# Sixteen modulation blocks as columns on TensorE: stationary weights and a one-column moving operand in place of a broadcast gate product

## The chip, the cores and the metric

The kernel runs on one NeuronCore of one Trainium2 chip. The metric is the device time in microseconds of one execution; three runs of the kernel before gave a median of 2649.09 us (2648.99 to 2653.47).

## What is computed

Two transformer stacks run one after the other on 256 positions of width 1024, in float32. The first stack has two layers with adaptive modulation; only its first layer matters here:

```python
c_act = silu(c)                                   # (1, 1024)
mod = c_act @ ada_w[i] + ada_b[i]                 # (1, 6144)
sh_m, sc_m, gt_m, sh_f, sc_f, gt_f = split(mod, 6)
h = rmsnorm(x, g0) * (1 + sc_m) + sh_m
y = rglru_mixer(h, ...)                           # layer 0
x = x + gt_m * rmsnorm(y, g1)                     # first gate
h = rmsnorm(x, g2) * (1 + sc_f) + sh_f            # shift and scale of the first conv FFN
y = conv_ffn(h, ...)
x = x + gt_f * rmsnorm(y, g3)
```

The 6144 modulation values of a layer are 48 blocks of 128: blocks 0 to 7 are `sh_m`, 8 to 15 `sc_m`, 16 to 23 `gt_m`, 24 to 31 `sh_f`, 32 to 39 `sc_f`, 40 to 47 `gt_f`. A block is a product of a 1024-vector with a 1024 by 128 piece of `ada_w`, 512 KB in float32.

## The kernel before, in words

**Products of the stacks.** Weights come from one packed array in chunks of 512 KB (`Weights._raw`, L360, tile `raw`, four buffers). Most are split into a high and a low part, `hi` by ScalarE (L372) and `lo` by VectorE (L373), in nine buffers each, and a product is three TensorE passes (L439 to L441 for `mm_b`, 512 moving columns; L446 to L448 for `mm_a`, 256 moving columns). A plain float32 matmul, as in the lines below, shows as two matmul records and two weight loads in the profile.

**Modulation blocks on VectorE.** `ada_step` (L502) loads a transposed 128 by 1024 block (L508, tile `adar`, two buffers, or `adag` where `more` is set) and makes one multiply with accumulation against `silu(c)` broadcast to 128 partitions (`cact`; L510). The result is one column of `dot[i]`. The factor 2 left out of `silu` is put right by 0.5 in `mods` (L521). Blocks 0 to 15 of layer 0 are made in `rg_x`, two per step of a loop over eight 128-row slices of the input, as they are needed. The rest are made in the background: `bg(n)` (L1012) spreads `DUE` blocks over a stage, 16 in the first stage (`rg`), 28 in the first conv FFN.

**The first gate on TensorE.** Blocks 16 to 23 are not made that way. `rg_x` transposes `cact` eight times (L577) and copies the result to `crep` (L578): the vector along the partitions, repeated over 128 columns. `gate0` (L598) then multiplies `crep` (stationary) with eight 128 by 1024 pieces of `ada_w` (tile `adag`, two buffers, L611), 512 moving columns at a time (L613, 16 matmuls, accumulating in two `y` banks), adds the bias with two matmuls of one partition (L616), and VectorE scales both halves with `norm_g` (L617) into `row0`, a row already spread over 128 partitions.

**Other gates** are made by `gate_row` (L619) from columns: eight diagonal tiles `dg` on VectorE (L632, two buffers), eight 128 by 128 float32 matmuls with a tile of ones (L633) and two copies on ScalarE (L634).

**The first stage, `rg` (L802).** In order: `rg_x`; the depthwise convolution of its result (L831, L833); a loop over four groups `g` that takes two steps of `gate0`, then two gate products of 16 matmul records each (L850), their tanh and exp, and background blocks; square roots and scans (L873 to L876); a loop over eight columns blocks `j` of the gate branch (`up`, L446 to L448, 24 records per `j`, GeLU L884, split L451 and L452); the output projection (L439 to L441); then `turn`, which uses the gate row at L654 and the next layer's shift and scale in `pre` (L686, L688).

**Order.** A scheduler orders each engine's queue by readiness in its own model and by program order; calls wrapped in `keep_in_program_order` stay in order among themselves. All loads go through SyncE's one queue. TensorE, VectorE and SyncE execute their queues in order, so what waits at the head holds what stands behind it.

Of the kernel before, what the change touches and what calls it, by code (L numbers as in the profile page):

```python
# [8 lines left out]
F32 = mybir.dt.float32  # L9
F32R = mybir.dt.float32r  # L10
I32 = mybir.dt.int32
AF = mybir.ActivationFunctionType
OP = mybir.AluOpType
# [3 lines left out]
D = 1024  # L17
# [11 lines left out]
OVER = 4  # L29
LEAD, LATE = 4, 7  # L30

DUE = {(0, 0): 16, (0, 1): 28, (1, 0): 18, (1, 1): 10}

# [33 lines left out]
def _rows(w):  # L69

    return np.concatenate([w[k * 128:(k + 1) * 128] for k in range(w.shape[0] // 128)], 1)
# [194 lines left out]
def _host(inputs, stages1, stages2):  # L266
    p = {k: np.asarray(v) for k, v in inputs.items()}
    arr = {}
    pieces = []
    for st in stages1 + stages2:  # L270
        pieces += _pieces_stage(st, p)
    arr["w"] = _pack(pieces)
    plan = [(k, a.shape[1]) for k, a in pieces]
    arr["x"] = np.ascontiguousarray(p["x"][0])
    cols = _Cols()
    if stages1:
        arr["c"] = np.ascontiguousarray(p["c"])
        order = {0: [j for k in range(8) for j in (k, 8 + k)] + list(range(16, 48)), 1: list(range(48))}
        ada = []
        for i in range(2):  # L280
            t = p["ada_w"][i].T.reshape(48, 128, D)
            ada.append(t[order[i]])
        arr["ada"] = np.ascontiguousarray(np.stack(ada))
        arr["adag"] = np.ascontiguousarray(p["ada_w"][0][:, 2 * D:3 * D]).reshape(8, 128, D)
        arr["gateb"] = np.ascontiguousarray(np.stack([p["ada_b"][0][2 * D:3 * D], p["norm_g"][0, 1]]))
        for i in range(2):
            cols.add(f"ada_b{i}", p["ada_b"][i])
            for n in range(4):
                cols.add(f"norm_g{i}{n}", p["norm_g"][i, n])
            for n in range(3):  # L290
                cols.add(f"cf_w{i}{n}", p["ffn_conv_w"][i, n])
            cols.add(f"cf_b{i}", p["ffn_conv_b"][i])
        for n in range(4):
            cols.add(f"rg_w{n}", p["rg_conv_w"][0, n])
        for nm in ("rg_conv_b", "rg_ba", "rg_bx", "rg_lambda", "gla_b_alpha"):
            cols.add(nm, p[nm][0])
        arr["walpha"] = np.ascontiguousarray(p["gla_w_alpha"][0])
        arr["gla_g"] = np.ascontiguousarray(p["gla_norm_g"])
        ii = np.arange(128)
        m = np.zeros((128, 8, 128), np.int32)  # L300
        for l in range(7):
            s = 64 >> l
            m[:, l, :] = ((ii[:, None] // (2 * s) == ii[None, :] // (2 * s))
                          & (ii[:, None] // s % 2 == 0) & (ii[None, :] // s % 2 == 1))
        m[:, 7, :] = np.eye(128, dtype=np.int32)
        arr["glamask"] = m
        arr["cols"] = np.ascontiguousarray(np.concatenate(cols.parts, 1))
    if stages2:
        arr["lngb"] = np.ascontiguousarray(np.stack([p["ln_g_2"], p["ln_b_2"]], 2).reshape(12, 2, D))
        arr["fox_b"] = np.ascontiguousarray(p["fox_b_f_2"])  # L310
        arr["mla_g"] = _colv(np.concatenate([p["mla_q_norm_g_2"][0], p["mla_kv_norm_g_2"][0]]))
        ii = np.arange(128)
        cm = np.zeros((128, 256), np.float32)
        cm[:, 128:] = np.where(ii[:, None] >= ii[None, :], 0.0, NEG)
        arr["cmask"] = cm
        arr["tri"] = (ii[:, None] <= ii[None, :]).astype(np.float32)
        tabs = []
        for dim in (16, 32):
            inv = np.float32(500000.0) ** (-np.arange(0, dim, 2, dtype=np.float32) / np.float32(dim))
            ang = np.arange(S, dtype=np.float32)[:, None] * inv[None, :].astype(np.float32)  # L320
            co, si = np.cos(ang), np.sin(ang)
            tabs.append(np.concatenate([co, co, -si, si], 1))
        arr["rope"] = np.ascontiguousarray(np.concatenate(tabs, 1).astype(np.float32))
    return arr, plan, cols.at
# [150 lines left out]
class Block1:  # L475
# [9 lines left out]
    def ada_init(self):  # L485
        nc, Q = self.nc, self.Q
        c = Q.tile([128, D], F32, name="cact")
        nc.sync.dma_start(out=c, in_=self.a["c"][0].partition_broadcast(128))
        self.cols = Q.tile([128, self.a["cols"].shape[1]], F32, name="cols")
        nc.sync.dma_start(out=self.cols, in_=self.a["cols"])  # L490
        th = Q.tile([128, D], F32, name="adar", tag="adar", bufs=2)
        self.ACT.activation(out=th, in_=c, func=AF.Tanh, scale=0.5)
        self.V.scalar_tensor_tensor(out=c, in0=th, scalar=1.0, in1=c, op0=OP.add, op1=OP.mult)
        self.cact = c
        self.dot = [Q.tile([128, 48], F32, name=f"dot{i}") for i in range(2)]
        self.mod = [Q.tile([128, 48], F32, name=f"mod{i}") for i in range(2)]
        self.order = {0: [j for k in range(8) for j in (k, 8 + k)] + list(range(16, 48)), 1: list(range(48))}

        self.todo = [(i, b) for i in range(2) for b in range(48) if i or not 16 <= b < 24]
        self.done = set()  # L500

    def ada_step(self, pin=False, more=False):  # L502
        if not self.todo:
# [56 lines left out]
    def rg_x(self):  # L560


        k, nc, V = self.k, self.nc, self.V
        xn = self.normed()
        xT = self.R.tile([128, 8, 256], F32, name="xnT", tag="big0", bufs=1)
        for kk in range(0, 8, 2):
# [2 lines left out]
                for t in range(2):  # L569
                    nc.tensor.transpose(p[:, q, t * 128:t * 128 + 128], xn[t][:, (kk + q) * 128:(kk + q + 1) * 128], k.ident)  # L570
            self.ACT.copy(out=xT[:, kk:kk + 2, :], in_=p)

        self.crep = self.R.tile([128, 8, 128], F32, name="crep", tag="crep", bufs=1)
        for q in range(0, 8, 4):
            p = k.bank("u", 4, (128, 4, 128))
            for j in range(4):
                nc.tensor.transpose(p[:, j, :], self.cact[:, (q + j) * 128:(q + j + 1) * 128], k.ident)  # L577
            self.ACT.copy(out=self.crep[:, q:q + 4, :], in_=p)  # L578
        acc = [k.bank("y" if j < 4 else "u", 4) for j in range(8)]
        h = self.h_tiles()  # L580
        mod, dot = self.mod[0], self.dot[0]
# [13 lines left out]
                    nc.tensor.matmul(acc[n * 4 + j][:, :256], w[:, j * 128:j * 128 + 128], f, start=kk == 0, stop=kk == 7)  # L595
        return h, acc

    def gate0(self):  # L598

        k, Q, R, nc = self.k, self.Q, self.R, self.nc  # L600
        two = R.tile([1, 128], F32, name="two", tag="two", bufs=1)
        self.V.memset(two, 2.0)
        b = Q.tile([1, D], F32, name="gb0", tag="xn", bufs=2)
        k.tc.keep_in_program_order(nc.sync.dma_start(out=b, in_=self.a["gateb"][0:1]))
        self.row0 = Q.tile([128, D], F32, name="grow", tag="grow", bufs=1)
        k.tc.keep_in_program_order(nc.sync.dma_start(out=self.row0, in_=self.a["gateb"][1].partition_broadcast(128)))
        p = [k.bank("y", 4) for _ in range(2)]
        half = [slice(n * 512, n * 512 + 512) for n in range(2)]
        for kk in range(8):
            w = R.tile([128, D], F32, name="adag", tag="adag", bufs=2)  # L610
            k.tc.keep_in_program_order(nc.sync.dma_start(out=w, in_=self.a["adag"][kk]))  # L611
            for n in range(2):
                nc.tensor.matmul(p[n], self.crep[:, kk, :], w[:, half[n]], start=kk == 0, stop=False)  # L613
            yield
        for n in range(2):
            nc.tensor.matmul(p[n], two, b[:, half[n]], start=False, stop=True)  # L616
            self.V.scalar_tensor_tensor(out=self.row0[:, half[n]], in0=p[n], scalar=0.5, in1=self.row0[:, half[n]], op0=OP.mult, op1=OP.mult)  # L617

    def gate_row(self, i, w):  # L619

        if (i, w) == (0, 0):
            return self.row0
        k, Q = self.k, self.Q
        m = self.mods(i, 3 * w + 2)
        gc = k.small("gc", 8)
# [176 lines left out]
    def rg(self):  # L802
# [32 lines left out]


        au = []
        gate0 = self.gate0()
        for g in range(4):
            gates = []  # L840
            next(gate0)
            next(gate0)
            for q, nm in enumerate(("wa", "wx")):
                w = k.whole(f"rg.{nm}.{g}")
                u = k.bank("u", 4, (128, 2, 256))
# [20 lines left out]
            V.scalar_tensor_tensor(out=xg, in0=ig, scalar=1.0, in1=xg, op0=OP.add, op1=OP.mult)  # L866
            au.append((d, r, xg))
            self.bg(6)
        for _ in gate0:
            pass  # L870
        for g in range(4):
            d, m, xg = au[g]
            k.tc.keep_in_program_order(ACT.activation(out=m, in_=m, func=AF.Sqrt, scale=-0.25))  # L873
# [4 lines left out]
        xhi = R.tile([128, 8, 256], F32R, name="xchi", tag="big1", bufs=1)  # L878
        xlo = R.tile([128, 8, 256], F32R, name="xclo", tag="big2", bufs=1)
        for j in range(8):  # L880
            u = k.bank("u", 4)
            self.up(u[:, :256], f"rg.g.{j}", x)
            ge = n2("wx")[:, :256]
            k.tc.keep_in_program_order(ACT.activation(out=ge, in_=u[:, :256], func=AF.Gelu_apprx_tanh))  # L884
            V.tensor_tensor(out=xc[:, j, :], in0=ge, in1=xc[:, j, :], op=OP.mult)
            k.split(xhi[:, j, :], xlo[:, j, :], xc[:, j, :])
            self.bg(24)
# [132 lines left out]
    def run(self):  # L1020
# [5 lines left out]
        for st in k.stages1:  # L1026
# [6 lines left out]
                self.pre(0, mods, x)  # L1033
                end = [1, mods, x]
            with k.tc.tile_pool(name=f"st_{st[0]}{i}", bufs=1) as self.R:
                k.pad(self.R, st[0], 40)
                stage = self.rg() if st[0] == "rg" else self.gla(x) if st[0] == "gla" else self.conv_ffn(i, x)
                if st[0] != "rg":

# [540 lines left out]
```

## Time and profile before

| | |
|---|---|
| median of three runs | 2649.09 us |
| the profiled execution | 2656.96 us |
| its span, first to last instruction | 2655.2 us |
| TensorE busy in the span | 98% |
| VectorE busy | 72% |
| ScalarE busy | 53% |
| bytes moved by DMA | 514.39 MB |

The profiled execution took 7.87 us (0.3%) more than the median; 1.8 us of its time lie outside the span. Busy time of TensorE is modelled (a matmul's end overlaps the next one's start), so the pace of matmuls is read from start to start, and idle time from the waits.

### The profile page before, as it was taken

Reading aid. Unit: us, or ns where it says so; the run is one execution under the profiler, and the core shown is the slowest. Engines: PE = TensorE matmul, PEld = TensorE weight load, DVE = VectorE, ACT = ScalarE, POOL = GpSimd, SP = SyncE. Lnnn points to the kernel's source line nnn. Section 1 sums busy time; section 2 is a strip of 40 time slices with the busy share of each in tenths; the row PEclk is TensorE's granted clock in tenths of the full one; section 3 lists DMA queues with packets and bytes.
Section 4 is the critical chain, followed back from the end, with each engine's and each line's share of the span. In section 5 each row is a group of like instructions: output and inputs, shape, how many; then the busy total and the mean of one; then the engine's idle time right before and its main releaser. Section 6 shows DMA issues by size and latency. Waiting matters only on the chain.

```text
span 2655.2 us, 44259 instructions
## 1 busy us (share of the span) xinstructions
PE 2591.1 (98%) x16680; PEld 2289.2 (86%) x16680; DVE 1918.3 (72%) x3876; ACT 1414.8 (53%) x2848; POOL 77.8 (3%) x115
## 2 busy tenths in 40 slices
PE   7899998999999999999999999999999999999998
PEld 5689887899899779989987899899889989977897
DVE  6889888887666886676666855766885676687755
ACT  4665564766554655444555544544754455456542
POOL 0000010000000000000000000000000000000000
PEclk9999999999999999999999999999999999999999
DMA  8878674665765537666654565665455565453652
GB/s 315 301 245 304 220 253 158 226 211 162 223 192 168 166 118 232 195 185 207 192 174 126 186 187 175 215 192 158 153 175 191 177 214 195 154 188 115 222 188 91
DMA packets 141082, 514.39 MB, mean 194 GB/s; under 512 B 16178, under 2 KB 16562, under 8 KB 139331
## 3 DMA queue, kind: packets, MB, share of 16 engines
q1 hardware_dynamic: 140866, 511.56, 59.9%
q8 instruction: 131, 2.15, 0.3%
q14 instruction: 85, 0.69, 0.1%
HBM read 510.44 MB, written 1.05 MB: 193 GB/s over the span
## 4 chain that ended last, share of the span: by engine, by line
PE 78%; DVE 8%; issue 8%; DMA 3%; ACT 2%; POOL 1%; DVEq 0%; POOLq 0%; SPq 0%; ACTq 0%
PE u L446 11%; PE u L448 11%; PE u L447 11%; PE y L441 10%; PE y L440 10%; PE y L439 10%; DVE lo L373 3%; PE u L439 2%; PE u L441 2%; PE u L440 2%; DMA raw<-w 2%; PE u L1232 1%; PE u L470 1%; PE u L1259 1%; PE u L1251 1%
## 5 line engine op out<-in xcount | busy, mean ns | idle before, releaser
L373 DVE TENSOR_TENSOR lo<-raw,hi 128x512 fp32r<-128x512 f32 (+4 forms) x1501 | 1080.8, 746 | 500.1 <-ACT hi L372 488.5
L372 ACT CAST hi<-raw 128x512 fp32r<-128x512 f32 (+4 forms) x1501 | 952.2, 667 | 735.3 <-issue 411.0
L446 PE MATMUL u<-hThi,hi 128*128 128x256 f32 x3016 | 841.1, 279 | 3.2 <-ACT hi L372 1.4
L447 PE MATMUL u<-hTlo,hi 128*128 128x256 f32 x3016 | 838.4, 278 | 0.0
L448 PE MATMUL u<-hThi,lo 128*128 128x256 f32 x3016 | 837.9, 278 | 0.2 <-DVE lo L373 0.2
L446 PEld LDWEIGHTS u<-hThi,hi 128*128 128x128 f32 x3016 | 566.8, 188 | 7.9 <-ACT hi L372 1.6
L447 PEld LDWEIGHTS u<-hTlo,hi 128*128 128x128 f32 x3016 | 567.2, 188 | 4.5 <-issue 1.0
L448 PEld LDWEIGHTS u<-hThi,lo 128*128 128x128 f32 x3016 | 568.9, 189 | 0.5 <-DVE lo L373 0.4
L441 PE MATMUL y<-hi,hT 128*128 128x512 f32 x704 | 276.9, 393 | 0.0
L440 PE MATMUL y<-lo,hT 128*128 128x512 f32 x704 | 276.5, 393 | 0.0
L439 PE MATMUL y<-hi,hT 128*128 128x512 f32 x704 | 274.4, 390 | 0.0
L439 PE MATMUL y<-hi,hThi 128*128 128x512 f32 (+6 forms) x504 | 189.5, 377 | 0.9 <-ACT hThi L451 0.8
L440 PE MATMUL y<-lo,hThi 128*128 128x512 f32 (+6 forms) x504 | 185.8, 370 | 0.0
L441 PE MATMUL y<-hi,hTlo 128*128 128x512 f32 (+6 forms) x504 | 185.0, 371 | 0.2 <-DVE hTlo L452 0.2
L440 PEld LDWEIGHTS y<-lo,hT 128*128 128x128 f32 x704 | 132.2, 188 | 27.4
L439 PEld LDWEIGHTS y<-hi,hT 128*128 128x128 f32 x704 | 132.2, 188 | 27.3
L441 PEld LDWEIGHTS y<-hi,hT 128*128 128x128 f32 x704 | 132.3, 188 | 27.0
L439 PE MATMUL u<-hi,hThi 128*128 128x512 f32 x320 | 127.2, 399 | 1.6 <-ACT hThi L451 1.6
L451 ACT CAST hT<-th 128x256 fp32r<-128x256 f32 x144 | 58.4, 406 | 130.5 <-DVE th L1119 130.5
L440 PE MATMUL u<-lo,hThi 128*128 128x512 f32 x320 | 125.5, 393 | 0.0
L441 PE MATMUL u<-hi,hTlo 128*128 128x512 f32 x320 | 124.5, 394 | 0.0
L439 PEld LDWEIGHTS y<-hi,hThi 128*128 128x128 f32 x504 | 94.9, 188 | 18.7 <-ACT hThi L451 2.3
(301 smaller groups left out, 3122.8 us busy)
## 6 DMA issues: line engine op xcount, KB each, us to landing
raw<-w SPq DMA_DIRECT2D x823, 512.0 KB, 3.8
adar<-ada SPq DMA_DIRECT2D x80, 512.0 KB, 4.8
gb<-lngb SPq DMA_DIRECT2D x12, 1024.0 KB, 4.8
adag<-ada SPq DMA_DIRECT2D x8, 512.0 KB, 5.4
adag<-adag SPq DMA_DIRECT2D x8, 512.0 KB, 6.2
raw<-w SPq DMA_DIRECT2D x8, 384.0 KB, 3.0
raw<-w SPq DMA_DIRECT2D x5, 480.0 KB, 3.7
raw<-w SPq DMA_DIRECT2D x4, 396.0 KB, 3.0
```

What stands on the lines that cost most here:

```text
L372: nc.scalar.copy(out=hi[:, a:b], in_=r[:, a:b])
L373: nc.vector.tensor_tensor(out=lo[:, a:b], in0=r[:, a:b], in1=hi[:, a:b].bitcast(F32), op=OP.subtract)
L439: mm(out, xhi, w[0], start=start, stop=False)
L440: mm(out, xhi, w[1], start=False, stop=False)
L441: mm(out, xlo, w[0], start=False, stop=stop)
L446: mm(out, whi, xhi, start=start, stop=False)
L447: mm(out, whi, xlo, start=False, stop=False)
L448: mm(out, wlo, xhi, start=False, stop=stop)
L451: self.nc.scalar.copy(out=hi, in_=src)
L470: self.nc.tensor.transpose(p[:, k * 128:k * 128 + 128], x[:, (h + k) * 128:(h + k + 1) * 128], self.ident)
L1232: nc.tensor.matmul(scores[e], qh(e), kh(e), start=True, stop=True)
L1251: nc.tensor.transpose(pt[:, e, j, :], probs[e0 + e][:, j * 128:j * 128 + 128], k.ident)
```

## The change

The product with `crep` goes, with its transposes, its copies, the bias matmuls and the bias and norm arrays. Blocks 16 to 31, the first gate and the shift of the first conv FFN, are made by TensorE as columns: `silu(c)` is held as eight columns (`ccol`), a block's 1024 by 128 piece of weights is the stationary operand, eight 128 by 128 tiles of it, and one column of `ccol` is the moving operand. Eight blocks share a PSUM bank and are copied to `dot` together. Eight blocks run in the loop over `g` (two per group), eight in the loop over `j` (one per column block). The first gate's row is made by `gate_row` at `j == 2`. VectorE's background share of the first stage falls from 16 blocks to 8.

```diff
-DUE = {(0, 0): 16, (0, 1): 28, (1, 0): 18, (1, 1): 10}
+PEADA = (16, 32)
+ROWAT = 2
+DUE = {(0, 0): 40 - PEADA[1], (0, 1): 28, (1, 0): 18, (1, 1): 10}
...
-        arr["adag"] = np.ascontiguousarray(p["ada_w"][0][:, 2 * D:3 * D]).reshape(8, 128, D)
-        arr["gateb"] = np.ascontiguousarray(np.stack([p["ada_b"][0][2 * D:3 * D], p["norm_g"][0, 1]]))
+        arr["adag"] = np.ascontiguousarray(np.stack([
+            _rows(p["ada_w"][0][:, j * 128:j * 128 + 128]) for j in range(PEADA[0], PEADA[1])]))
...
+        cols.add("c", p["c"][0])
...
-        self.todo = [(i, b) for i in range(2) for b in range(48) if i or not 16 <= b < 24]
-        self.done = set()
+        self.ccol = Q.tile([128, 8], F32, name="ccol")
+        self.ACT.activation(out=self.ccol, in_=self.col("c", 0, 8), func=AF.Tanh, scale=0.5)
+        self.V.scalar_tensor_tensor(out=self.ccol, in0=self.ccol, scalar=1.0, in1=self.col("c", 0, 8), op0=OP.add, op1=OP.mult)
+        self.todo = [(i, b) for i in range(2) for b in range(48) if i or not PEADA[0] <= b < PEADA[1]]
+        self.done, self.rows = set(), {}
...
-        self.crep = self.R.tile([128, 8, 128], F32, name="crep", tag="crep", bufs=1)
-        for q in range(0, 8, 4):
-            p = k.bank("u", 4, (128, 4, 128))
-            for j in range(4):
-                nc.tensor.transpose(p[:, j, :], self.cact[:, (q + j) * 128:(q + j + 1) * 128], k.ident)
-            self.ACT.copy(out=self.crep[:, q:q + 4, :], in_=p)
...
-    def gate0(self):
...
+    def pe_ada(self):
+
+        k, nc = self.k, self.nc
+        p = None
+        for j in range(*PEADA):
+            w = self.R.tile([128, D], F32, name="adag", tag="adag", bufs=2)
+            k.tc.keep_in_program_order(nc.sync.dma_start(out=w, in_=self.a["adag"][j - PEADA[0]]))
+            if j % 8 == 0:
+                p = k.bank("y", 4, (128, 512))
+            for kk in range(8):
+                nc.tensor.matmul(p[:, j % 8:j % 8 + 1], w[:, kk * 128:kk * 128 + 128], self.ccol[:, kk:kk + 1], start=kk == 0, stop=kk == 7)
+            if j % 8 == 7:
+                self.V.tensor_copy(self.dot[0][:, j - 7:j + 1], p[:, :8])
+                self.done |= {(0, b) for b in range(j - 7, j + 1)}
             yield
...
     def gate_row(self, i, w):
 
-        if (i, w) == (0, 0):
-            return self.row0
+        if (i, w) in self.rows:
+            return self.rows.pop((i, w))
...
-        gate0 = self.gate0()
+        pe = self.pe_ada()
         for g in range(4):
             gates = []
-            next(gate0)
-            next(gate0)
+            next(pe)
+            next(pe)
...
-        for _ in gate0:
-            pass
...
         for j in range(8):
+            next(pe, None)
+            if j == ROWAT:
+                self.rows[0, 0] = self.gate_row(0, 0)
             u = k.bank("u", 4)
             self.up(u[:, :256], f"rg.g.{j}", x)
...
-                k.pad(self.R, st[0], 40)
+                k.pad(self.R, st[0], 24)
```

## Rows read from the trace of the kernel before

**Rows 1.** The page's first part: busy time of each engine in the span.

```profile
PE 2591.1 (98%) x16680; PEld 2289.2 (86%) x16680; DVE 1918.3 (72%) x3876; ACT 1414.8 (53%) x2848; POOL 77.8 (3%) x115
```

**Rows 2.** Stretches: us, busy PE, PEld, DVE, ACT, POOL; granted clock, DMA share, GB/s.

```profile
50.50:84.00 33.50, 27.63 (x91) 17.78 (x89) 25.33 (x47) 22.99 (x47) 0.00 (x0) 0.90 0.83 303
84.00:140.00 56.00, 51.22 (x304) 42.07 (x303) 51.32 (x81) 31.48 (x53) 3.42 (x6) 1.00 0.86 293
340.00:2655.20 2315.20, 2282.66 (x14859) 2025.35 (x14857) 1632.43 (x3355) 1220.44 (x2523) 64.62 (x85) 1.00 0.57 182
```

**Rows 3.** What TensorE waited for, 50 to 84 us, then 84 to 140 us.

```profile
PE y L613 <- DMA adag<-adag: 4.9, 1, 4.9
...
PE u L682 <- DVE xn L677: 1.7, 1, 1.7
PE y L440 <- DVE lo L373: 1.6, 3, 1.0
PE u L446 <- ACT hi L372: 1.4, 1, 1.4
```

**Rows 4.** TensorE's instructions in order of time (start, us, line, count, idle before).

```profile
50.56 3.65 PE L613 MATMUL y<-adag,crep 128*128 128x512 f32 x8
58.74 3.60 PE L613 MATMUL y<-adag,crep 128*128 128x512 f32 x8
62.18 10.52 PE L850 MATMUL u<-xc,raw 128*128 128x256 f32 x48
77.57 6.75 PE L613 MATMUL y<-adag,crep 128*128 128x512 f32 x8 [4.87 <-DMA adag<-adag]
83.76 0.68 PE L446 MATMUL u<-hThi,hi 128*128 128x256 f32 x1
...
95.22 1.98 PE L616 MATMUL y<-gb,two 1*128 1x512 f32 x4
97.13 0.38 PE L447 MATMUL u<-hTlo,hi 128*128 128x256 f32 x1
```

**Rows 5.** SyncE's queue in order of time, then median landing time of those loads.

```profile
64.91 4.70 SPq L360 DMA_DIRECT2D raw<-w  x3
70.53 0.90 SPq L611 DMA_DIRECT2D adag<-adag  x2
...
adag<-adag SPq DMA_DIRECT2D x8, 512.0 KB, 6.2
```

**Rows 6.** Weight loads in order of time, two products of 16 moving columns.

```profile
1380.19 0.42 PEld L1426 LDWEIGHTS u<-lf,ones 128*128 128x128 f32 x2
1380.54 0.30 PEld L1427 LDWEIGHTS u<-lf,tri 128*128 128x128 f32 x2
1380.76 0.19 PEld L439 LDWEIGHTS y<-hi,hThi 128*128 128x128 f32 x1
```

**Rows 7.** Weight loads in order of time: at full clock, then at half clock.

```profile
400.91 1.87 PEld L969 LDWEIGHTS u<-F 128*128 128x128 f32 x16
402.70 0.19 PEld L441 LDWEIGHTS y<-hi,hTlo 128*128 128x128 f32 x1
...
436.11 3.12 PEld L971 LDWEIGHTS u<-qT,kT 128*128 128x128 f32 x16
```

**Rows 8.** VectorE: one block, the gate's last step, and the diagonal tiles.

```profile
96.43 1.22 DVE L510 SCALAR_TENSOR_TENSOR adar<-adar,cact 128x1024 f32<-128x1024 f32 x1
97.58 1.28 DVE L617 SCALAR_TENSOR_TENSOR grow<-y,grow 128x512 f32<-128x512 f32 x2
...
L632 DVE TENSOR_SCALAR dg<-ident,gc x24: 277/286/290, 277.7 to 654.1; 128x128 f32<-128x128 f32 x24
```

**Rows 9.** A stretch behind TensorE's wait (columns as in group 2).

```profile
78.00:80.00 2.00, 2.00 (x3) 0.75 (x3) 2.00 (x4) 0.48 (x1) 0.00 (x0) 0.50 0.75 240
```

**Rows 10.** ScalarE in order of time: copies of the vector, the next step.

```profile
15.45 1.12 ACT L578 COPY crep<-u 128x512 f32<-128x512 f32 x2 [0.27 <-PE u L577]
17.28 0.60 ACT L555 ACTIVATE hf<-xnT,mod,A 128x256 f32<-128x256 f32 x1 [0.71 <-DVE lam L818]
```

More of the change, by code (lines that the diff above doesn't have):

```diff
@@ L596, in rg_x @@
         return h, acc
-    def gate0(self):
[L600 to L613, printed above, removed]
+    def pe_ada(self):
[11 more added lines that the diff above has]
+                self.done |= {(0, b) for b in range(j - 7, j + 1)}
             yield
-        for n in range(2):
-            nc.tensor.matmul(p[n], two, b[:, half[n]], start=False, stop=True)
-            self.V.scalar_tensor_tensor(out=self.row0[:, half[n]], in0=p[n], scalar=0.5, in1=self.row0[:, half[n]], op0=OP.mult, op1=OP.mult)
     def gate_row(self, i, w):
-        if (i, w) == (0, 0):
-            return self.row0
+        if (i, w) in self.rows:
+            return self.rows.pop((i, w))
         k, Q = self.k, self.Q
```

## The prediction, made before the changed kernel was run

> **What bounds the kernel now.** I read the page's busy times first, then the busy times by stretch, then what TensorE waited for, then its instructions in order of time. The reader should see that TensorE is the bound nearly everywhere: 98% busy over the span [rows 1], and after 340 us 2282.7 of 2315.2 us [rows 2]. A delay of TensorE in the first stage has no slack behind it that could take it up, so it arrives at the end nearly whole.
>
> The change touches two stretches. From 50.5 to 84 us (the loop over `g`) TensorE's work and gaps alternate: three pairs of gate steps, the four group products, and one wait of 4.87 us for a load of `adag`, after which the engine ran its eight records from 77.57 to 83.76 us instead of in some 3.4 us [rows 4]; the granted clock in that stretch is 0.50, the 1.2 GHz level [rows 9]. From 84 to 140 us (the loop over `j`, the output projection, the first turn) TensorE waited 1.7 + 1.6 + 1.4 us and some tenths [rows 3]; the rest is back-to-back work. VectorE is 51.3 of 56 us busy there [rows 2], about as full, but TensorE's waits on it are only the 1.7 + 1.6 us. So work put on TensorE here costs its full length, and work taken from VectorE gives back at most the waits.
>
> **What goes from TensorE.** Sixteen gate matmuls of 512 columns show as 32 records. A pair of steps is eight records; from 58.74 to 62.18 us that is 3.44 us, 0.43 us each [rows 4]. At full clock 32 x 0.43 = 13.8 us. The bias matmuls run from 95.22 to 97.13 us, 1.9 us [rows 4]. Together 15.7 us. The eight transposes and, behind them, the two copies of the vector end before 17.28 us, where ScalarE's next step waited 0.71 us for VectorE [rows 10]: they lie beside other work and count nothing either way. In the same place the new tanh and multiply on eight columns are two tiny instructions; I count 0, at most some tenths.
>
> **What comes to TensorE.** Sixteen blocks of eight float32 matmuls are 128 matmuls, 256 records, each with a fresh 128 by 128 weight load. No row has one moving column. The nearest has 16: its four weight loads run from 1380.19, with the third at 1380.54 and the next line's at 1380.76, so 0.11 us from load to load [rows 6]. With 128 columns it is (402.70 - 400.91) / 16 = 0.112 us [rows 7]. The pace does not fall from 128 columns to 16, so the weight load sets it and one column should not help: 256 x 0.112 = 28.7 us. The ends: 0.06 us a record if the load can be had at about half that price (nothing here shows it), 15.4 us; and 0.195 us, the pace of the same shapes at half clock (3.12 / 16) [rows 7], 49.9 us. I take 0.112, which both rows give.
>
> The Trainium skill, page "TensorE: Matmul & The Clock Gate", section "Back-to-back issue gap", puts a matmul of 1 to 64 columns at about 25 ns; by that the blocks would be an estimated 256 x 0.025 = 6.4 us. The loads of [rows 6] speak against it at 0.11 us, and the same page's section on LDWEIGHTS makes the load depend on its columns alone, which the trace agrees with. The sum doesn't use it.
>
> The row at `j == 2` adds eight 128-column float32 matmuls, 16 records, 16 x 0.112 = 1.8 us. Its diagonal tiles come two at a time from VectorE at 0.29 us each [rows 8]; if VectorE is late TensorE waits. I add 0.7 us for that, 0 to 3.
>
> So TensorE's own work grows by 28.7 + 1.8 - 15.7 = **14.8 us**.
>
> **What VectorE and the loads give back.** VectorE loses eight blocks at 1.15 us each (96.43 to 97.58, where the next line starts) and the gate's last step, 1.2 us [rows 8], 10.4 us; it gains eight diagonal tiles at 0.25 to 0.29 us and five tiny steps, about 3 us. The net 7 us matters only through TensorE's waits. The bytes stay: eight loads of 512 KB move from VectorE's blocks to TensorE's, and one broadcast of 512 KB goes. Their place changes: in the loop over `g` SyncE has some five fewer `adar` loads ahead of or among the `adag` loads. In the kernel before the third pair was issued only at 70.53 us, behind three `raw` loads that held the queue 4.70 us, and landed 7 us later [rows 4, 5]. Fewer loads that wait for VectorE should bring it earlier. What can come back: the wait, 4.9 us, the half-clock excess, 6.2 - 3.4 = 2.7 us, and up to 3.2 us of waits on `hi` and `lo` between 84 and 140 us: 10.8 us in all. Half of the first two and a third of the last is my value, 3.8 + 1.0 = 4.8 us, 0 and 10.8 the ends; the `raw` loads still hold the queue.
>
> Then the sum: 14.8 + 0.7 - 4.8 = **+10.7 us**, taken as +10. Against the profiled execution that is 2656.96 + 10 = 2667; that execution is 7.9 us over the median of the runs, so in the metric 2649.1 + 10 = **2659 us**. The ends of this case: 14.8 - 10.8 = +4 and 14.8 + 0.7 = +15.5, 2653 to 2665.
>
> **Queues that are moved past.** SyncE is the one to watch. In the loop over `j` it now has eight `adag` loads between the weight loads. Each waits until TensorE has finished the block two before it, and behind it stand the `raw` loads that feed `hi` and `lo`. Block to block is 24 records at 0.117 us plus 1.8 us, 4.6 us, so a load has 2 x 4.6 - 1.8 = 7.4 us to land; the median landing is 6.2 us [rows 5]. It fits, with little to spare. VectorE's copy of eight columns and the row's tiles stand in its queue among the splits; the row is used only at the turn, after the output projection, and the shift later still, so neither is late. GpSimd's queue is not touched.
>
> **Rivals.**
>
> *One: the clock falls in the blocks.* One moving column for each load leaves the array almost without work, and a pair of blocks in the loop over `g` is 3.6 us long. After the wait of 4.87 us the clock was at 0.50 for the next six microseconds [rows 4, 9]. If a stretch of one-column matmuls is treated like a wait, the blocks go from 0.112 to 0.195 us a record: half of them so is 128 x 0.083 = +11 us on top of the first sum, 2670; all, with the group products behind them slowed, some +25 us, 2684. Against it: the engine is never without an instruction, and single blocks in the loop over `j` stand between dense products. 18%.
>
> *Two: a new wait takes the place of the old.* TensorE meets a block whose load has not landed. The price of one such wait is in the trace: 4.9 us and 2.7 us of half clock. Two more of them than I counted give 2659 + 15 = 2674; eight waits of 1 us give 2667. The 7.4 us against 6.2 us above is what decides. 12%.
>
> *Three, the other side: the record is cheaper than its load looks.* If a record costs c, TensorE's growth is 272c - 15.7 (with the row at the same pace), and with all 10.8 us given back the change breaks even at c = 26.5 / 272 = 0.097 us and is faster by more than 0.2% (5.3 us) below 0.078 us. At 0.06 us it is 16.3 - 15.7 - 10.8 = -10 us, 2639. For it: every load in the trace stands beside at least 16 columns, and VectorE, relieved by 7 us where it is 92% busy, may free more than the waits I can see. Against it: rows 6 and 7 give the same pace at 16 and 128 columns. By the Trainium skill's 25 ns (the same section) it would end at an estimated 2631. 22%: 14 with the time below -0.2%, 8 within.
>
> **How the numbers follow.** First sum 48%, rivals 18, 12 and 22%. About 0.2% of the time, 5.3 us, is what a measurement of this kernel can tell from no change. Of the first sum 8 points lie below +5.3 us. So faster 0.14, same 0.08 + 0.08 = 0.16, slower 0.40 + 0.18 + 0.12 = 0.70. The range runs from 2640 (leaving out the far half of the third rival) to 2675 (leaving out the upper part of the first).
>
> **What would show it.** In the profile after: the 256 one-column records at 0.11 us from load to load, in blocks of 1.8 us; the loop over `j` longer by some 14 us, from its first L446 product to the output projection; VectorE no longer full there; the wait for `adag` near 72 us shorter. Loads at 0.2 us would show the first rival, idle time of TensorE ended by `adag` the second. The forecast is wrong if records come well under 0.1 us, or if the stretch from 50.5 us to the first turn is not longer than now: then TensorE was not what bound it.

## The result, and the profile after

The changed kernel is slower: a median of 2677.07 us (2668.25 to 2681.09, six runs) against 2650.43 us of the kernel before (2648.99 to 2653.47, six runs), a ratio of 1.0094 [1.0081, 1.0107], some +25 us (the two medians alone differ by 26.6 us). The forecast was 2659 us, with a range up to 2675: the sign is right, the time lies 2 us above the range, and +10 us was less than half of the loss.

The page of the kernel after gives busy time, share and instructions of each engine; it answers to [rows 1].

```profile
PE 2609.9 (98%) x16908; PEld 2317.8 (87%) x16908; DVE 1912.1 (72%) x3870; ACT 1414.9 (53%) x2849; POOL 76.7 (3%) x115
```

TensorE has 18.8 us more, the share is the same 98%, and 228 more records came to it. The two stretches of [rows 2], for the kernel after (us, busy PE, PEld, DVE, ACT, POOL; granted clock, DMA share, GB/s):

```profile
50.50:84.00 33.50, 32.46 (x177) 29.51 (x176) 17.34 (x35) 15.28 (x35) 0.00 (x0) 0.80 0.68 249
84.00:140.00 56.00, 54.08 (x377) 52.39 (x377) 36.54 (x66) 27.48 (x42) 0.00 (x0) 0.85 0.64 227
```

TensorE is now nearly full in both, and VectorE went from 51.3 to 36.5 us of 56. But the granted clock fell from 0.90 and 1.00 to 0.80 and 0.85. What TensorE still waited for, 50 to 84 us and then 84 to 160 us, beside [rows 3]:

```profile
PE y L608 <- DMA adag<-adag: 1.0, 1, 1.0
...
PE u L450 <- ACT hi L376: 1.7, 1, 1.7
PE u L677 <- DVE xn L672: 0.9, 1, 0.9
PE y L444 <- DVE lo L377: 0.2, 1, 0.2
```

That is 3.8 us. Before it was 10.8 us with two smaller waits that [rows 3] leaves out (1.0 and 0.2). So the waits shrank as hoped, and yet the first transpose of the turn stands 20.4 us later, the kernel before first:

```profile
136.79 1.09 PE L682 MATMUL u<-ident,xn 128*128 128x128 f32 x8 [1.67 <-DVE xn L677]
...
157.21 1.09 PE L677 MATMUL u<-ident,xn 128*128 128x128 f32 x8 [0.92 <-DVE xn L672]
```

That is the loss of this stage. TensorE's instructions in order of time (start, us, line, count, idle before) show how the new blocks went; the group products (L850 in [rows 4]) are L845 here:

```profile
50.46 4.11 PE L608 MATMUL y<-ccol,adag 128*128 128x1 f32 x32
55.61 3.57 PE L608 MATMUL y<-ccol,adag 128*128 128x1 f32 x16 [1.04 <-DMA adag<-adag]
59.05 6.04 PE L845 MATMUL u<-xc,raw 128*128 128x256 f32 x16
64.92 1.84 PE L608 MATMUL y<-ccol,adag 128*128 128x1 f32 x16
66.63 3.70 PE L845 MATMUL u<-xc,raw 128*128 128x256 f32 x16
70.17 3.63 PE L608 MATMUL y<-ccol,adag 128*128 128x1 f32 x32
73.66 8.84 PE L845 MATMUL u<-xc,raw 128*128 128x256 f32 x32
```

At full clock a block of 16 one-column records runs from 64.92 to 66.63, 1.71 us, 0.107 us a record. The block at 55.61 takes 3.44 us to the next line, 0.215 us a record. And 16 group products take 3.5 us from 66.63 on, but 5.9 us from 59.05 on. The granted clock around the first block:

```profile
50.00:52.00 2.00, 2.00 (x17) 1.78 (x17) 2.00 (x6) 1.40 (x4) 0.00 (x0) 1.00 0.89 358
52.00:54.00 2.00, 2.00 (x18) 2.00 (x18) 2.00 (x6) 0.00 (x0) 0.00 (x0) 0.89 0.40 147
54.00:56.00 2.00, 0.96 (x5) 0.88 (x6) 2.00 (x6) 0.00 (x0) 0.00 (x0) 0.50 0.54 199
```

TensorE was busy without a gap from 50 to 54 us, and the clock fell, from 2.4 to 1.2 GHz, inside that: the first 32 records need 4.11 us and not 3.4. The wait of 1.04 us for `adag` comes only behind the fall. The same happened right behind the block that ends at 73.66 us, and in the gapless block that begins at 98.92 us:

```profile
74.00:76.00 2.00, 2.00 (x7) 1.53 (x6) 1.26 (x3) 0.00 (x0) 0.00 (x0) 0.51 0.67 262
...
100.00:102.00 2.00, 2.00 (x17) 2.00 (x17) 2.00 (x7) 1.07 (x3) 0.00 (x0) 0.84 0.57 186
```

A fourth fall, at 87.7 us, stands 1.8 us behind a wait of 1.68 us for `hi`.

The span of this profiled execution is 11.3 us over that of before, less than 20.4 us. The rest came back in two later stretches that the change leaves alone: lined up instruction by instruction, the execution after makes up some 5 us between 1505 and 1660 us and 4 us from 2500 us on. wide64 (below) makes up neither and gate_wide64_row7 both, so this does not belong to the change. The execution after is also the quickest of its six. So size is judged by the medians, and place by the stage.

### The profile page after: what moved, and what is told of

Read it like the earlier page. It is cut to its first block, busy times and chain, and to the rows that moved or that the text cites. A ratio compares the mean times of both kernels' runs of the same rounds, so it can differ in the third digit from the quotient of the medians.

```text
span 2666.5 us, 44709 instructions
## 1 busy us (share of the span) xinstructions
PE 2609.9 (98%) x16908; PEld 2317.8 (87%) x16908; DVE 1912.1 (72%) x3870; ACT 1414.9 (53%) x2849; POOL 76.7 (3%) x115
## 4 chain that ended last, share of the span: by engine, by line
PE 82%; DVE 9%; DMA 3%; issue 3%; ACT 2%; POOL 1%; DVEq 0%; SPq 0%; POOLq 0%; ACTq 0%
PE u L450 11%; PE u L451 11%; PE u L452 11%; PE y L445 11%; PE y L444 10%; PE y L443 10%; DVE lo L377 3%; PE u L443 3%; PE u L445 3%; PE u L444 3%; DMA raw<-w 2%; DVE adar L517 1%; PE u L474 1%; PE u L1228 1%; PE y L608 1%
```

## The experiments

All kernels below are the changed kernel with the edits shown, and each ratio is against the kernel before on the same chip. Two theories stood against each other for what the forecast had missed: the clock (one column for each load leaves the array so little work that the clock falls) and the passes (the added weight loads cost more than counted, or new waits came in). The number of columns tells them apart, since it leaves the loads as they are.

### The same blocks with 64 equal columns: wide64

```diff
+        self.crep = self.R.tile([128, 8, 64], F32, name="crep", tag="crep", bufs=1)
+        self.ACT.copy(out=self.crep, in_=self.ccol[:, :, None].to_broadcast([128, 8, 64]))
...
-                nc.tensor.matmul(p[:, j % 8:j % 8 + 1], w[:, kk * 128:kk * 128 + 128], self.ccol[:, kk:kk + 1], start=kk == 0, stop=kk == 7)
+                nc.tensor.matmul(p[:, j % 8 * 64:j % 8 * 64 + 64], w[:, kk * 128:kk * 128 + 128], self.crep[:, kk, :], start=kk == 0, stop=kk == 7)
...
```

The copy to `dot` then takes the first of each block's 64 equal columns.

> The changed kernel with one edit: the moving operand is the same column repeated 64 times (64 columns for each 128 by 128 weight load instead of one); column 0 of the result is used. The number of weight loads stays 256, and at 0.107 us from load to load 64 columns in two passes should still fit behind a load. Clock theory (a stretch of one-column matmuls is taken like idle time and TensorE falls to its 1.2 GHz level): the granted clock of 50.5 to 140 us goes from 0.80 to 0.85 back to 0.95 or more, and the time falls from about 2677 to about 2660 us, leaving the added passes. Pass theory (the loss is the added passes and their place in the queue alone): the clock and the time stay, 2673 to 2681 us. If wider operands cost time of their own, records would be longer than 0.11 us and the time above 2681 us.

Measured: 2665.9 us (2660.42 to 2669.99, four runs), ratio 1.0052 [1.0032, 1.0071]. Its blocks and its group products (L847) in order of time:

```profile
51.15 3.74 PE L610 MATMUL y<-crep,adag 128*128 128x64 f32 x32
55.80 3.69 PE L847 MATMUL u<-xc,raw 128*128 128x256 f32 x16 [0.92 <-issue]
59.33 3.68 PE L610 MATMUL y<-crep,adag 128*128 128x64 f32 x32
62.85 3.67 PE L847 MATMUL u<-xc,raw 128*128 128x256 f32 x16
...
145.76 1.10 PE L679 MATMUL u<-ident,xn 128*128 128x128 f32 x8 [1.62 <-DVE xn L674]
```

From 59.33 to 62.85 us 32 records take 3.52 us, 0.110 us each: 64 columns cost what one column costs (0.107 us), so it is the weight load that sets the pace. The last row is the turn: 145.8 us, 9.0 us behind the kernel before and 11.4 us ahead of the one-column kernel. One row for the whole part from 48 to 150 us tells the clock: kernel after, then wide64, then the kernel before.

```profile
48.00:150.00 102.00, 99.04 (x608) 91.95 (x607) 64.40 (x114) 50.73 (x90) 0.67 (x3) 0.85 0.69 246
...
48.00:150.00 102.00, 94.99 (x641) 87.83 (x640) 71.64 (x127) 58.60 (x106) 2.51 (x6) 0.97 0.77 273
...
48.00:150.00 102.00, 91.36 (x450) 70.03 (x449) 87.08 (x143) 63.40 (x114) 6.57 (x12) 0.97 0.83 288
```

A mean clock of c with two levels means half clock for 2 x (1 - c) of the time: 30.6 us with one column, 6.1 us in the other two. Work that runs at half clock loses half of that time, so the one-column form loses (30.6 - 6.1) / 2 = 12.2 us in this part (the clock has two digits, so that is good to about 1 us). The difference of the two ratios, 1.0094 - 1.0052, is 11 us with an uncertainty of some 6. The clock is no accident of the profiled executions: over the whole span it is 0.987 to 0.991 in all six runs of the kernel after, and 0.995 or 0.996 in all four of wide64. What is left, 1.0052, some +14 us, is put down to the added passes less the waits. So the clock theory held for the clock, and for about half of the loss; the time stayed 6 us above the 2660 us that it gave.

### Sixteen columns: wide16

The same edit with 16 in place of 64.

> The changed kernel (sixteen blocks, row at j == 2) with 16 moving columns. The records stay at 0.107 us, set by the weight load. Clock theory: the clock follows how much the array is fed, so 16 columns lie between 1 (about 2675 us) and 64 (about 2666 us); if even 16 count as little, it is with the first, 2670 to 2678 us and a granted clock below 0.9 from 50 to 84 us. Pass theory: 2666 to 2675 us whatever the width, with no order in the clock.

Measured: 2671.72 us (2665.3 to 2681.68), 1.0081 [1.0058, 1.0104]. Its row of the same part:

```profile
48.00:150.00 102.00, 98.69 (x575) 93.66 (x576) 59.08 (x108) 47.20 (x86) 0.00 (x0) 0.78 0.65 227
```

0.78 is 45 us at half clock, more than with one column. Here the first fall stands behind a wait of 1.59 us for `adag`, so the extra 14 us are not put down to the columns. But two later falls, at 74.0 and 111.6 us, lie in gapless work with 16-column blocks, as with one column. What follows is only that 16 columns do not keep the clock where 64 did.

### Half of the change: gate_cols and gate_wide64

Only the eight blocks of the gate on TensorE; the shift's eight blocks stay on VectorE. With one column, and with 64.

```diff
-PEADA = (16, 32)
+PEADA = (16, 24)
```

> The changed kernel with eight blocks instead of sixteen on TensorE as columns (the first gate only, blocks 16 to 23); VectorE keeps the shift's eight, 16 background blocks as before the change. TensorE's own work is then about that of the kernel before: 128 records x 0.107 + 16 x 0.11 for the row = 15.5 us against 15.7 us. Pass theory: the loss goes with the passes, so the time comes back to 2650, plus or minus 4 us. Clock theory: the loop over groups keeps its one-column stretches, so some 8 us of half clock stay there: 2655 to 2662 us.

> Both edits: eight blocks only, and 64 moving columns. Clock theory: no added passes and no half clock, so 2645 to 2651 us, at or below the kernel before, and 6 to 12 us below the run with one column and eight blocks. Pass theory: the same as that run, within 3 us.

Measured: 2670.54 us (2663.28 to 2675.99), 1.0069 [1.0047, 1.0091], with one column; 2659.22 us (2658.22 to 2664.17), 1.0035 [1.0024, 1.0046], with 64. By the ratios the columns cost some 9 us again; by the medians gate_wide64 is 11 us below gate_cols, where the pass theory had them equal. But half of the blocks did not halve the rest: gate_cols lies above both of its ranges, gate_wide64 8 us above that of the clock theory. Part of the reason is a wait that the kernel after does not have; TensorE in gate_wide64:

```profile
104.93 1.22 PE L630 MATMUL u<-dg,ones 128*128 128x128 f32 x4 [12.34 <-DVE dg L629]
```

With eight blocks the row at `j == 2` comes up sooner, and its diagonal tiles stand in VectorE's queue behind scans, splits and background blocks. The prediction had given that 0 to 3 us; here it is 12.3 us (10.2 us in gate_cols), and the clock is down through nearly all of it. So both are spoiled as a measure of half the change, and the row was moved.

### No block on TensorE: all_dve

```diff
-PEADA = (16, 32)
+PEADA = (16, 16)
...
-        pe = self.pe_ada()
...
-            next(pe)
-            next(pe)
...
-            next(pe, None)
```

> No block on TensorE: all 48 of layer 0 are made by VectorE (24 background blocks in the first stage), the first gate's row from columns as in the changed kernel. TensorE loses 15.7 us of gate products and gets 1.8 us for the row; VectorE gets 9.2 us more than before the change. If TensorE alone bounds the first stage: 2650 - 13.9 plus small waits, 2636 to 2643 us. If VectorE is as much a bound there (92% busy from 84 to 140 us before the change): its 8 us of added work show as TensorE's waits on lo and on the scans, 2644 to 2655 us. Slower than 2655 us would say that VectorE, not TensorE, set the pace of the stage.

Measured: 2664.09 us (2663.21 to 2667.58), 1.0049 [1.0034, 1.0064]; the wait for the diagonal tiles is 19.9 us. Spoiled in the same way.

### The row at the end of the loop: four kernels

```diff
-ROWAT = 2
+ROWAT = 7
```

in the kernel after (after_row7), and with the eight gate blocks of one column (gate_cols_row7), of 64 columns (gate_wide64_row7), and with none (all_dve_row7).

> The changed kernel with the row at j == 7. In the changed kernel TensorE showed no wait for the row's tiles, but the row's matmuls were split over 14 us in the middle of a stretch at half clock. Clock theory: the blocks stay what they are, so 2668 to 2680 us. If the row's place is the cause of the loss: 2655 to 2664 us, with the clock near full.

> Eight blocks, one moving column, row at j == 7. Clock theory: slower than the same with 64 columns by 4 to 10 us, with a lower granted clock from 50 to 84 us. Pass theory: within 3 us of it.

> Eight blocks on TensorE, 64 moving columns, and the gate's row made at j == 7 instead of j == 2. In the run with the row at j == 2 TensorE stood 12.3 us waiting for the row's first diagonal tiles, which VectorE had behind its scans and splits. If that wait is the loss there (2659 us): the wait goes and the time is 2644 to 2652 us, at or below the kernel before. If eight blocks as columns cost more than the eight steps they replace: 2655 us or more.

> No block on TensorE, row at j == 7. The run with the row at j == 2 had one wait of 19.9 us for the row's tiles, and half clock behind it. TensorE-bound theory: without it 2636 to 2645 us. VectorE-bound theory (24 background blocks in the first stage are too much for it): waits on lo and on the split of the gate branch take the wait's place, 2650 us or more.

| kernel | median us (runs) | ratio |
|---|---|---|
| after_row7 | 2673.95 (2668.04 to 2678.42) | 1.0075 [1.0056, 1.0095] |
| gate_cols_row7 | 2670.14 (2661.92 to 2672.4) | 1.0057 [1.0037, 1.0077] |
| gate_wide64_row7 | 2655.36 (2652.86 to 2662.27) | 1.0010 [0.9998, 1.0021] |
| all_dve_row7 | 2659.85 (2656.66 to 2664.74) | 1.0023 [1.0014, 1.0033] |

**after_row7**: the interval overlaps with that of the change, and its granted clocks in the two stretches are 0.80 and 0.85 as well. The row's place has no part in what the change cost that these runs could tell.

**gate_cols_row7 and gate_wide64_row7** are the closest pair in order: from their first block at 51 us on, TensorE runs a block of 32 records, 16 group products and a second block of 32 in both, and both come out of a dip of the clock with full clock. Their second block and the group products behind it, one column first:

```profile
61.17 4.56 PE L608 MATMUL y<-ccol,adag 128*128 128x1 f32 x32
65.59 13.01 PE L845 MATMUL u<-xc,raw 128*128 128x256 f32 x48
...
60.95 3.68 PE L610 MATMUL y<-crep,adag 128*128 128x64 f32 x32
64.47 10.58 PE L847 MATMUL u<-xc,raw 128*128 128x256 f32 x48
```

And the stretches of 2 us over it, one column first:

```profile
61.00:63.00 2.00, 2.00 (x20) 1.97 (x18) 0.75 (x2) 1.54 (x4) 0.00 (x0) 1.00 0.59 207
63.00:65.00 2.00, 2.00 (x15) 2.00 (x14) 2.00 (x4) 0.00 (x0) 0.00 (x0) 0.66 0.53 203
65.00:67.00 2.00, 2.00 (x7) 1.75 (x8) 1.43 (x3) 0.00 (x0) 0.00 (x0) 0.50 0.62 213
...
61.00:63.00 2.00, 2.00 (x20) 2.00 (x19) 0.69 (x2) 1.77 (x5) 0.00 (x0) 1.00 0.69 217
63.00:65.00 2.00, 2.00 (x18) 1.95 (x18) 2.00 (x5) 0.00 (x0) 0.00 (x0) 1.00 0.42 158
65.00:67.00 2.00, 2.00 (x11) 1.77 (x10) 1.50 (x3) 0.55 (x2) 0.00 (x0) 1.00 0.59 193
```

TensorE is 2.00 of 2.00 us busy in all six, with nearly the same loads. With one column the clock falls during the block; with 64 it stays. The block itself loses 0.9 us (4.42 against 3.52, start to next line), and the 48 dense products behind it 2.4 us: the larger part of the price is paid by what comes after. By the ratios the pair differs by 1.0057 - 1.0010, some 12 us, a little more than the 4 to 10 us expected, and the granted clock over the span is 0.987 to 0.991 in the runs of one form and 0.993 to 0.995 in those of the other.

One stretch of this pair does not show the cause by itself, for a block of one column need not bring the clock down. gate_cols has the same 32 records and the same products behind them, and the clock stays at 1.00:

```profile
60.03 3.63 PE L608 MATMUL y<-ccol,adag 128*128 128x1 f32 x32
63.52 10.61 PE L845 MATMUL u<-xc,raw 128*128 128x256 f32 x48
...
62.00:64.00 2.00, 2.00 (x17) 1.97 (x18) 2.00 (x4) 0.00 (x0) 0.00 (x0) 1.00 0.44 168
64.00:66.00 2.00, 2.00 (x11) 1.74 (x11) 1.32 (x3) 0.47 (x2) 0.00 (x0) 1.00 0.73 231
```

There the block began 1.2 us after the clock had risen from a dip; in gate_cols_row7 it began 0.9 us after, in gate_wide64_row7 1.5 us. What decides in which block the clock falls is not shown. What the traces do show is the count between 48 and 150 us. Falls with no wait of TensorE above 0.1 us in the 6 us before them: with one column three in the kernel after, four in after_row7, one in gate_cols_row7, none in gate_cols; with 16 columns two; with 64 columns none in the four kernels, although gate_early (below) has the longest blocks of all, 48 records without a gap, twice, at 1.00.

**gate_wide64_row7** itself, at 2655.36 us, lies in the second range of its expectation. But the kernel before had a median of 2653.31 us on that chip, and the ratio, 1.0010 [0.9998, 1.0021], cannot be told from no change. With the wait for the row's tiles gone and less of the clock lost, eight blocks as columns cost about what the eight steps cost that they replace.

**all_dve_row7** was to show what the passes on TensorE cost. It has no gate work on TensorE at all, 75 us busy of the 102 from 48 to 150 us, and is still slower than the kernel before. Its waits there, and its clock:

```profile
PE u L448 <- ACT wx L874: 6.4, 1, 6.4
PE u L450 <- DVE lo L375: 4.7, 2, 2.4
PE u L840 <- issue: 4.5, 1, 4.5
PE y L442 <- DVE lo L375: 4.0, 2, 3.4
PE u L675 <- DVE xn L670: 3.4, 2, 2.2
...
48.00:150.00 102.00, 75.11 (x390) 64.91 (x389) 87.75 (x156) 57.79 (x105) 4.25 (x6) 0.85 0.72 250
```

TensorE now stands for VectorE and ScalarE, and 4.5 us for nothing that the profile shows, and behind these gaps the clock is down for as long as in the kernel after. So in this stage work taken from TensorE does not come back whole: part of it had filled time in which the engine would have waited.

### Loads of the eight blocks earlier: gate_early

In gate_wide64_row7 TensorE waited 1.75 us for `adag` and 5.9 us for `hi`. A third buffer and an earlier turn were to take the first away. The edit against that kernel (`ada_step` names the same tile, with three buffers too):

```diff
-            w = self.R.tile([128, D], F32, name="adag", tag="adag", bufs=2)
+            w = self.R.tile([128, D], F32, name="adag", tag="adag", bufs=3)
...
-            next(pe)
-            next(pe)
+            for _ in range((3, 3, 2, 0)[g]):
+                next(pe)
```

> Eight blocks, 64 columns, row at j == 7, and their loads earlier: three buffers for adag instead of two, blocks taken 3, 3, 2 in the first three groups instead of 2, 2, 2, 2. It removes the wait for adag (1.7 us) and the two blocks from the loop over j. If TensorE bounds the loop over j: 3 to 6 us less than with row at j == 7 alone, 2647 to 2653 us, below or at the kernel before. If waits on hi and lo (8.5 us in that run) come last there, TensorE only waits longer for them and the time stays at 2653 to 2658 us.

Measured: 2655.54 us (2651.51 to 2663.16), 1.0019 [1.0008, 1.0030]: no gain, as the second half of the expectation has it. The two blocks that ran at 88.97 and 91.34 us, in the loop over `j`, now run at 77.68 and 80.47 us. The wait for `adag` is still 1.0 us, and TensorE reaches the products of the loop over `j` before their weights are split. Its two long blocks, and the waits from 48 us to the turn:

```profile
51.90 5.53 PE L610 MATMUL y<-crep,adag 128*128 128x64 f32 x48
60.78 5.47 PE L610 MATMUL y<-crep,adag 128*128 128x64 f32 x48
...
PE u L450 <- ACT hi L376: 10.5, 5, 7.1
```

The wait on `hi` went from 5.9 to 10.5 us: the wait removed came back as another. No kernel tried was faster than the one before.

## Why the prediction was right, and where it was wrong

**Direction, and the weight loads: right.** The forecast of +14.8 us for TensorE's own work took 0.112 us a record. At full clock it is 0.107 us, with one column as with 64: 256 x 0.107 + 1.8 - 15.7 = 13.5 us. The pace that [rows 6, 7] gave for 16 and 128 columns held down to one, and the third rival, a cheaper record, fell. The far end of that term was misread: 0.195 us came from a stretch that ended at full clock again (438 to 440 us before has a granted clock of 0.82), and at half clock a record takes 0.215 us. The Trainium skill, page "TensorE: Matmul & The Clock Gate", section "LDWEIGHTS (loading the stationary operand)", gives columns / 1.2 in ns, 107 ns for 128, and the trace agrees; the 25 ns of its section "Back-to-back issue gap" were never met here.

**The waits: right in size, and partly by luck.** The wait for `adag` went from 4.9 to 1.0 us and all waits up to the turn from 10.8 to 3.8 us. But TensorE was also slower in the kernel after, so that what it needed had longer to arrive: with the clock kept, in wide64, the waits are 6.9 us, 3.0 of them for `adag`. The 3.9 us that came back there are the fairer measure of the forecast 4.8 us. The loads fitted in the kernel after: the median landing is 3.3 us after issue.

```profile
adag<-adag SPq DMA_DIRECT2D x16, 512.0 KB, 3.3
```

The second rival, new waits, had no part in the kernel after.

**The first sum as a whole** is what wide64 shows: at the clock of before the stage is 13.5 us of passes less 3.9 us of waits (10.8 to 6.9 us), +9.6, and its turn is 9.0 us late. By the ratio it is +14 us, with 8.5 to 19 by the interval; the forecast's +10.7 lies within.

**The step that failed is "against it: the engine is never without an instruction", in the first rival.** That sentence carried the 18%, and the first sum took all 256 records, and the products behind them, at full clock. It took the clock to follow the gaps. But [rows 9] showed the clock only behind a wait, and no row of before had a stretch of TensorE's with loads and next to no moving columns; the case was not bounded by a row, it was argued away. In the kernel after the clock fell three times inside gapless work, each time with one-column blocks running or just done, and half clock cost 12.2 us on top of the first sum. The mechanism was written down and priced; that 11 us for "half of them" is close to the 12.2 us found is luck. Not half of the records ran at half clock but the blocks at 55.61 and 105.99 us and parts of three others, 10.2 us in all, some 48 of the 256 records. That is a loss of 5.1 us; the larger part of the 12 us fell on the products behind, which the 11 us left out.

The stage adds up: 13.5 us of passes and 12.2 us of clock less 7.0 us of waits is 18.7 us, against 20.4 us at the turn; 1.7 us stay unexplained.

**Median against profiled execution.** The six runs of the kernel after have granted clocks over the whole span of 0.987 to 0.991, the profiled one 0.991; the runs of the kernel before mostly 0.995 and 0.996; wide64 0.995 and 0.996. Half of 2 x (0.995 - 0.991) x 2667 is 11 us for the profiled execution, and with the median 0.989 it is 16 us. So a lower clock accounts for some 5 us of the 9 us between profiled execution and median, as far as three digits carry it. Where in the other runs the clock fell further is not known: they have no trace.

**"Work put on TensorE here costs its full length"** held for this change, but the reverse, that work taken off comes back, did not: all_dve_row7 has 24 us less busy time there than the kernel after and its turn is only 10 us earlier, still 10 us later than the kernel before:

```profile
147.00 1.11 PE L675 MATMUL u<-ident,xn 128*128 128x128 f32 x8 [2.25 <-DVE xn L670]
```

The prediction's picture of one bound was too simple. In the loop over `g` the gate's passes also covered waits: ahead of the first group product TensorE stands 4.5 us in all_dve_row7, with the clock down from 54.0 us, and 1.0 us in the kernel before, at 1.00.

**Still open.** Among widths the scheduler's order differs in detail behind the first block; in the closest pair it is the same from the first block to the fall, while wide64 and the kernel after differ from their second block on. The price of the columns is therefore taken from two pairs (11 and 12 us, each with an uncertainty of some 6), not from one. Why one block brings the clock down and another like it does not is open. Whether 32 columns would do was not tried.

## What to carry to other kernels

A float32 vector product with stationary weights costs two records with a weight load each for every 128 by 128 tile, 0.107 to 0.110 us a record here at full clock with 1, 16 and 64 columns alike. So fewer columns buy nothing; repeat the moving column (64 equal columns here) so that a long run of loads is less likely to pull the clock down for the dense work behind it. Before calling an engine "never idle, so its clock is safe", look for a stretch of the same shape at full clock in the trace; where there is none, the clock is an open term with a price on both sides. One such stretch is no proof either: gate_cols kept the clock in a block like those that lost it in the kernel after. And an engine that is 98% busy over the span can still be filling time in one stage: see what it would wait for there before counting its work as savings.

## What was not expected of the hardware

The granted clock of TensorE fell from 2.4 to 1.2 GHz in a stretch without any idle time, with one moving column for each 128 by 128 float32 load: 1.00 to 0.50 within the 4.11 us of the first 32 records, and in gate_cols_row7 at 63 to 65 us, where 64 columns kept 1.00. It does not happen in every such block: in gate_cols the clock stayed at 1.00 through 32 records from 60.03 us on. At 1.2 GHz the load is slower as well, 0.215 us a record against 0.107. Sixty-four columns are no guard against gaps: in gate_wide64_row7 and in its one-column twin the clock was down alike behind a wait of 0.92 and 0.97 us near 55 us, while in wide64 it stayed at 1.00 behind the same 0.92 us. In gate_wide64 it fell at 89.8 us inside a block of 64 columns, 2.3 us behind a wait of 0.86 us.
